# Gate stores on ScalarE's queue, respaced key and value products, state rows at another place, and one bias product for four heads

## The chip, the cores and the metric

The kernel runs on one core of a Trainium2 chip. The core has TensorE (PE, with PEld for its weight loads), VectorE (DVE), ScalarE (ACT), GpSimd (POOL) and SyncE (SP), and 16 DMA engines that move data between DRAM and on-chip memory. DMAs are issued here from SP's queue, from POOL's and, in places, from ACT's. The metric is the device time of one execution in microseconds. The kernel before took 2555.72 us in the median of three runs (2555.23 to 2556.82).

## The reference

The kernel computes one layer of a hybrid mixer for a prompt of 2048 rows and for 64 sample rows (8 sequences of 8 new rows each, with cached keys and values). The parts that the change touches are these:

```python
z = einsum('btd,de->bte', rms_norm(x, g_norm), w_in)          # one wide product, cut into
xa, ga, q, k, v, gb, gm = split(z, [o1, o2, o3, o4, o5, o6])  # recurrence, attention, gates
xa, new_conv = causal_conv(xa, conv_buf, conv_w, conv_b)      # new_conv is an output
hs, h_last = rg_lru(xa, h0, ...)                              # h_last is an output
for g in range(3):                    # windows 128, 512, 2048; dilations 1, 4, 16; 4 heads each
    bias = rel_bias[t5_bucket(arange(129) * DILATIONS[g]), g * 4:(g + 1) * 4]
    # prompt: 128 queries against 256 keys in the band, score * scale + bias[distance]
    # sample: 64 queries, each against 129 keys of its cache, then P @ cached values
    o, lse, nb = dilated_group(q[g], k[g], v[g], cache[g], bias, DILATIONS[g])
alpha = softmax(stack(lses), axis=0)                          # merges the three groups
yb = einsum((sum(alpha * outs) * silu(gb)), w_attn_proj)
gates = sigmoid(gm + b_merge)                                 # 2 x 1024 columns
merged = gates[..., :1024] * ya + gates[..., 1024:] * yb
y = x + einsum(merged, w_out)
```

## The kernel before, in words

Everything is written out by hand: each engine executes its list in the order in which the program emits it, and an instruction that waits holds all that stand behind it on its engine. The same holds for each engine's list of DMA issues. The hardware DMAs, from SP and from ACT alike, use eight semaphores in turn, so a DMA also waits until the one that last used its semaphore has landed.

A product of full precision is three matmul passes: the 24 matmuls of `zT` (line 757 on) take eight slices of the depth and, for each, the high weight part with the high input part, the low part with the high one, and the high one with the low input part (RH, RL).

*The attention stage* (64 to 1134 us of the trace) goes through 12 heads (groups 2, 1, 0), each in 17 units `ph`, one per 128 rows. In the unit loop the weights of the next head `nh` are loaded and converted, and its bias is made: `bias_0` (ph 7) loads the one-hot table of the group and lets POOL broadcast one column of `reln` to 128 columns, `bias_a` (ph 9) multiplies the two on PE to 128 equal rows of 383 values, copies them on ACT and stores them in the DRAM table `Dsc`, and `bias_b` (ph 12) loads two skewed views of it as the tile T. The first head's come at unit 0.

*The recurrence stage* (1134 to 1659 us) makes the recurrent branch. Its last block is finished inside the next stage.

*The gate stage* (1659 to 2078 us) goes over 16 blocks `f` of 128 gate columns (`gm_block`, line 991 on). A block is five chunks of 512, 512, 384, 384 and 320 rows. In each chunk PE makes the product z, hooks run, ACT makes the gate tile `gt` (sigmoid; two buffers in the blocks from 1 on), the tile is stored to DRAM (`Gsc`), and one piece of the cache is copied (`copy`). z takes turns in a few PSUM tiles, so PE waits when ACT has not emptied an old one. The weights of block f+1 are split into a high and a low part on ACT and DVE in chunk 0 of block f (`nextw`), and the raw weights of f+2 are loaded (`nextr`, line 680) into a single buffer, which that split has just read.

From block 1 on, each chunk then also does a step t of `plan` (line 1268 on), a table of lists of functions: the attention of the sample rows. Step t stands in chunk 6 + t, counted from the stage's start. In it are:
- the key products: `G.kq.go`, two products of 128 x 128 on DVE for each call; `kts` lists the steps of the calls (four a step from step 2, three from 20 to 23), and `kl` is the step behind the last;
- the multiplications of cached values: `v2_load` (SP, line 1152), `v2_mul` (ACT, four per tile, line 1156), `v2_acc` (DVE), and the like for group 1, spread over steps 6 to 66; a load goes out some four tiles ahead into six buffers;
- the products of the remaining values, `v_conv(i)` (ACT and POOL split a tile) and one step later `v_mm(i)` (PE, tile OT, line 1221), at the steps `mmt`, every second from `kl + 7`;
- the small tables `SA` (scores, lines 1062 and 1065), the queries `qs`, softmax and merge steps.

The state rows of the recurrence (`states`) are made by a hook in the last chunk of block 0: PE transposes the columns `par`, the last of which POOL writes (lines 927 and 928), DVE copies them, and SP stores four outputs. The tile `hs` lies where block 0's pools end.

*The output stage* (2078 us to the end) projects the attention, merges and multiplies by the last weights.

The functions that the diff touches, and what calls them:

Of the kernel before, what the change touches and what calls it, by code (L numbers as in the profile page):

```python
# [11 lines left out]
F32 = mybir.dt.float32  # L12
# [30 lines left out]
def program(tc, I, O, C, upto=99, debug=False):  # L43
# [13 lines left out]
    else:  # L57
        sd = lambda n, s, dt=F32: dram.tile(s, dt, name=n)
    Dsc = sd("Dsc", [12, 128, NBX])
    Osc = sd("Osc", [3, SEQ, 4, 130])  # L60
    QS = sd("QS", [3, NS, 512])
    SK = sd("SK", [3, NS, 2, 4, HD])
# [212 lines left out]
    heads = [(g, h) for g in (2, 1, 0) for h in range(4)]  # L275
    Wt, Wr, Tt = {}, {}, {}

    def bias_0(g, h):
        hd = g * 4 + h
        oh = ap_.tile([128, NBX], F32, name="oh", tag="wraw", bufs=4)  # L280
        dma(oh[0:33, :], C["onehot"][:, g, :])
        lb = ap_.tile([128, HD], F32, name="lb", tag="kqs", bufs=1)
        POOL.tensor_copy(lb[0:33, :], reln[:, hd:hd + 1].to_broadcast([33, 128]))
        G.ohlb = oh, lb

    def bias_a(g, h):
        hd = g * 4 + h
        oh, lb = G.ohlb
        eb = ps.tile([128, NBX], F32, name="eb", tag="op")
        PE.matmul(eb, lb[0:33, :], oh[0:33, :], start=True, stop=True)  # L290
        es_ = ap_.tile([128, NBX], F32, name="es_", tag="wraw", bufs=4)
        ACT.copy(es_, eb)
        dma(Dsc[hd], es_)

    def bias_b(g, h):
        hd = g * 4 + h
# [202 lines left out]
    x_mul(1, D // 2, D)  # L499
    POOL.tensor_scalar(gq, gq, -SCALE, 0.0, ALU.mult, ALU.add)  # L500
    POOL.tensor_scalar(reln[0:32, :], reln[0:32, :], -1.0, 0.0, ALU.mult, ALU.add)
    bias_0(*heads[0])
    w_conv(heads[0], 6, DVE)
    w_conv(heads[0], 7, DVE)
    N = len(units)
# [30 lines left out]
    for i in range(N + 3):  # L536
# [82 lines left out]
        if u:  # L619
            if i < 15:  # L620
                x_mul(i + 2, 0, D // 2)
            if i > 50 and i // 17 in (3, 7) and ph < 16:
                x_mul(ph, 0, D // 2)
            if i == 0:
                bias_a(*heads[0])
                bias_b(*heads[0])
        if nh:
            if ph == 7:
                bias_0(*nh)
            if ph == 9:  # L630
                bias_a(*nh)
            if ph == 12:
                bias_b(*nh)
            if ph == 11:
                for k in range(4):
                    w_load(nh, k)
            if ph == 13:
                w_conv(nh, 0, POOL)
                w_conv(nh, 1, DVE)
                w_load(nh, 4)  # L640
                w_load(nh, 5)
# [257 lines left out]
    def tail_2(b):  # L899
        for c0, n in CH:  # L900
            s = slice(c0, c0 + n)
            ACT.activation(rr[:, s], rr[:, s], AF.Exp, scale=c8[:, b:b + 1])
            a2 = lp.tile([128, 512], F32, name="a2", tag="ii", bufs=2)
            POOL.tensor_mul(a2[:, 0:n], rr[:, s], rr[:, s])
            DVE.scalar_tensor_tensor(tt[:, s], a2[:, 0:n], 1.0, tt[:, s], ALU.add, ALU.mult)

    def tail_r(b):
        for c0, n in CH:
            ACT.activation(tt[:, c0:c0 + n], tt[:, c0:c0 + n], AF.Sqrt)

    def tail_3(b, i0=0, i1=5):
        for c0, n in CH[i0:i1]:
            s = slice(c0, c0 + n)
            DVE.tensor_mul(xc[:, s], xc[:, s], tt[:, s])
            if c0 + n == NT:
                a0 = rr[:, SEQ:NT:8]
                hh = lp.tile([128, 8], F32, name="hh", tag="hh")
                DVE.tensor_mul(hh, a0, par[:, b, 34:42])
                DVE.tensor_add(xc[:, SEQ:NT:8], xc[:, SEQ:NT:8], hh)
                DVE.memset(a0, 0.0)  # L920
            init = 0.0 if c0 == 0 else tt[:, c0 - 1:c0]
            DVE.tensor_tensor_scan(tt[:, s], rr[:, s], xc[:, s], init, ALU.mult, ALU.add)
            POOL.tensor_mul(sgl[:, s], sgl[:, s], tt[:, s])
            dma(Y1[b][:, s], sgl[:, s])
        if i1 < 5:
            return
        POOL.tensor_copy(par[:, b, 4:5], tt[:, SEQ - 1:SEQ])
        POOL.tensor_copy(par[:, b, 34:42], tt[:, SEQ + 7:NT:8])
# [46 lines left out]
        POOL.tensor_copy(par[:, b, 0:3], xpad[:, SEQ:SEQ + 3])  # L975
        POOL.tensor_copy(par[:, b, 10:34].rearrange("p (s j) -> p s j", j=3), xsp[:, :, 8:11])

    def states():
        hs = lp.tile([42, 1024], F32, name="hs", tag="xh")
        for i in range(2):  # L980
            hp = ps.tile([42, 512], F32, name="hp", tag="tr")
            for k in range(4):
                PE.transpose(hp[:, k * 128:(k + 1) * 128], par[:, i * 4 + k, :], ident)
            DVE.tensor_copy(hs[:, i * 512:(i + 1) * 512], hp)
        for a, b, d in ((0, 3, O["conv_p"][0, 0]), (4, 5, O["h_p"][0]), (10, 34, O["conv_s"][0].rearrange("b j d -> (b j) d")), (34, 42, O["h_s"][0])):
            dma(d, hs[a:b, :])


    mg = ExitStack()
    tasks = []  # L990
# [1 line left out]
    def gm_block(f, w, hooks, gtile):  # L992
        for ci, (c0, n) in enumerate(CH):
            z = ztile("z", "S")
            zT(z, w, c0, n)
            for h in hooks.get(ci, ()):
                h()
            gt = gtile()
            ACT.activation(gt[:, 0:n], z[:, 0:n], AF.Sigmoid, bias=par[:, f % 8, 8 + f // 8:9 + f // 8])  # L999
            dma(Gsc[f][:, c0:c0 + n], gt[:, 0:n])  # L1000
            copy()
            if plan and f:
                for fn in plan.pop(0):
                    fn()
# [4 lines left out]
    def nextw(f):  # L1009
        if f + 1 < 16:  # L1010
            wm[f + 1] = w_split(G.wr, DVE)

    def nextr(f):
        if f + 2 < 16:
            G.wr = w_raw(wcols(C_GM + (f + 2) * 128))

    G.wr = wgr
    gm_block(0, wm[0], {0: (lambda: nextw(0), lambda: nextr(0), lambda: tail_2(7)), 1: (lambda: tail_r(7), lambda: tail_3(7, 0, 2)), 2: (lambda: tail_3(7, 2, 5),), 4: (states,)},
             lambda: lp.tile([128, 512], F32, name="gt0", tag="ii", bufs=2))
    lr.close()  # L1020
    gts = ExitStack()
# [34 lines left out]
    def sload(g):  # L1056
        SA = SAs[g] = mp.tile([NS, 4, 192], F32, name="SA", tag="SA", bufs=2)
        br = SA[:, :, 0:128]
        o = g * 4 * 128 * NBX + 127
        if g == 0:  # L1060
            for h in range(4):
                dma(br[:, h], raw(Dsc, o + h * 128 * NBX, [[0, 8], [NBX - 1, 8], [1, 128]]))
        else:
            dma(br, raw(Dsc, o, [[0, NS], [128 * NBX, 4], [1, 128]]))
        dma(SA[:, :, 128:192], SN[g * 4:g * 4 + 4].rearrange("h p k -> p h k"))
# [185 lines left out]
    def s_out2():  # L1251
# [7 lines left out]
        for a in range(2):  # L1259
            nc.gpsimd.dma_start(Y2v[:, a * 4:a * 4 + 4, SEQ:NT], yt[:, a])  # L1260

    sload(2)
    sload_k(2)
    prep()
# [8 lines left out]
    P = lambda f, *a: lambda: f(*a)  # L1273
    kts = []
    while len(kts) < G.kq.left:
        t = kts[-1] if kts else 2
        kts.append(t + (kts.count(t) == (3 if 20 <= t < 24 else 4)))
    kl = kts[-1] + 1
    mmt = [kl + 7 + 2 * i for i in range(NI_)]
    for i, (g, b, r) in enumerate(items):  # L1280
        if b is None and i:
            at_(mmt[i] - 1, P(s_evac, items[i - 1][0]), P(soft_b, g))
# [2 lines left out]
    for i in range(NI_):  # L1285
        at_(mmt[i] - 1, P(v_conv, i))
    T = mmt[-1]
    at_(1, G.kq.init, G.kq.queries)
    at_(2, P(scores, 2), P(news, 2, range(4)), P(sload, 1), P(sload_k, 1))
    at_(3, P(soft_a, 2))  # L1290
    at_(4, v2_p)
# [301 lines left out]
```

## Time and profile before

| | |
|---|---|
| median of three runs | 2555.72 us (2555.23 to 2556.82) |
| profiled execution | 2556.18 us |
| its span in the trace | 2554.4 us |
| PE busy | 2493.1 us (98%) |
| DVE busy | 1546.4 us (61%) |
| ACT busy | 1081.5 us (42%) |
| POOL busy | 557.9 us (22%) |
| DMA, mean | 147 GB/s |
| chain that ended last, share of PE | 83% |

The trace is of the profiled execution. Its times are microseconds from the start of the span; the span begins and ends a little inside the execution, which here adds 1.8 us. Busy time of an engine is the time in which it executes; idle time is followed by the name of what released it ("<-"). The granted clock is that of PE: 1.00 is 2.4 GHz and 0.50 is 1.2 GHz. A line number is that of the kernel's file; L93 and L94 are the two steps of a split into high and low parts, made by a helper for many tiles.

### The profile page before, as it was taken

The numbers are of one execution on the slowest core, as the hardware profiler recorded it, in microseconds if no ns is written. First come the engines' busy times: TensorE is split into PE (matmuls) and PEld (weight loads), VectorE is DVE, ScalarE is ACT, GpSimd is POOL, SyncE is SP. The second block draws the span as 40 slices with busy tenths as digits, with TensorE's granted clock in tenths as the row PEclk, the third lists the DMA queues.
The fourth block names the chain that finished last, engine by engine and source line by source line (L and its number), as shares of the span: only waits on it lengthen the run. The fifth ranks groups of instructions, "written<-read, shape, count | busy, mean of one in ns | idle before, by whom it ended". The sixth has DMA issues, their size and how long they took to land.

```text
span 2554.4 us, 44714 instructions
## 1 busy us (share of the span) xinstructions
PE 2493.1 (98%) x15196; PEld 2340.1 (92%) x15196; DVE 1546.4 (61%) x4805; ACT 1081.5 (42%) x3327; POOL 557.9 (22%) x897
## 2 busy tenths in 40 slices
PE   8999999999999999999999999999889999999999
PEld 7999999999999999999999999988778899988988
DVE  6744686777786776647676677638755723433322
ACT  5534454443454443444455655536466511211110
POOL 3423322222221221213233334320000012200000
PEclk9999999999999999999999999999999999999999
DMA  5443564554553433327644434355555479633332
GB/s 145 117 130 97 139 193 135 164 163 136 162 153 110 120 117 99 107 73 233 208 143 140 129 118 133 125 173 177 177 166 186 146 223 337 192 112 123 111 122 66
DMA packets 311288, 376.73 MB, mean 147 GB/s; under 512 B 54914, under 2 KB 254926, under 8 KB 308220
## 3 DMA queue, kind: packets, MB, share of 16 engines
q1 hardware_dynamic: 297028, 356.31, 45.7%
q0 software_dynamic: 14032, 17.57, 2.5%
q8 instruction: 120, 1.97, 0.3%
q14 instruction: 108, 0.88, 0.1%
HBM read 293.55 MB, written 168.31 MB: 181 GB/s over the span
## 4 chain that ended last, share of the span: by engine, by line
PE 83%; DMA 6%; DVE 5%; ACT 3%; issue 1%; SPq 1%; POOL 1%; DVEq 0%; ACTq 0%; POOLq 0%
PE z L336 28%; PE zt L760 22%; PE zt L1471 7%; PE zt L1503 7%; PE zt L534 3%; PE zt L1415 3%; PE zga L888 2%; DMA v<-in_cache_kv_w 2%; PE trx L247 1%; PE op L428 1%; PE S L406 1%; DVE kjk L178 1%; PE tre L416 1%; DMA xt<-in_x_prompt 1%; PE trc L376 1%
## 5 line engine op out<-in xcount | busy, mean ns | idle before, releaser
L336 PE MATMUL z<-w,RH 128*128 128x384 f32 (+1 forms) x3088 | 889.1, 349 | 6.1 <-POOL w L317 2.3
L760 PE MATMUL zt<-RH,wz 128*128 128x384 f32 (+2 forms) x2560 | 700.1, 356 | 12.9 <-ACT gt L999 12.0
L336 PEld LDWEIGHTS z<-w,RH 128*128 128x128 f32 (+1 forms) x3088 | 553.3, 188 | 16.1 <-POOL w L317 6.2
L336 PE MATMUL z<-w,RL 128*128 128x384 f32 x1544 | 520.5, 337 | 0.0
L760 PEld LDWEIGHTS zt<-RH,wz 128*128 128x128 f32 x2560 | 465.6, 190 | 58.8 <-ACT gt L999 14.2
L760 PE MATMUL zt<-RL,wz 128*128 128x384 f32 (+2 forms) x1280 | 454.1, 355 | 0.0
L336 PEld LDWEIGHTS z<-w,RL 128*128 128x128 f32 x1544 | 291.5, 189 | 0.7 <-DVE RL L94 0.4
L178 DVE CUSTOM_DVE_ANT_0 kjk<-kt,qs 128x128 bf16<-128x128 f32 x768 | 227.6, 296 | 63.1 <-DMA qs<-QS 27.7
L760 PEld LDWEIGHTS zt<-RL,wz 128*128 128x128 f32 x1280 | 242.4, 189 | 22.5
L408 ACT ACTIVATE P<-P,o 128x128 f32<-128x128 f32 (+1 forms) x192 | 88.9, 463 | 309.1 <-DVE o L407 309.1
L345 ACT ACTIVATE jk<-z 128x128 bf16<-128x128 f32 (+1 forms) x408 | 113.0, 277 | 236.5 <-PE trc L376 173.5
L94 DVE TENSOR_TENSOR KQ<-trc,KQ 128x256 fp32r<-128x256 f32 x192 | 81.4, 424 | 209.0 <-ACT KQ L93 209.0
L347 POOL TENSOR_SCALAR ss<-ss 128x2 f32<-128x2 f32 (+1 forms) x204 | 43.8, 215 | 714.5 <-ACT jk L345 671.2
L1471 PEld LDWEIGHTS zt<-y1t,w_wlo 128*128 128x128 f32 x1536 | 190.3, 191 | 0.6
L1471 PE MATMUL zt<-y1t,w_wlo 128*128 128x256 f32 (+1 forms) x1536 | 190.6, 286 | 0.0
L1503 PE MATMUL zt<-w_wo,mt 128*128 128x512 f32 x672 | 162.0, 395 | 0.0
L1503 PEld LDWEIGHTS zt<-w_wo,mt 128*128 128x128 f32 x672 | 126.1, 188 | 30.6
L348 POOL TENSOR_TENSOR rs<-ss,neghalf 128x2 f32<-128x2 f32 (+1 forms) x204 | 142.7, 699 | 17.0
L1156 ACT ACTIVATE v<-v,P 128x128 f32<-128x128 f32 x256 | 81.2, 391 | 77.7 <-DMA v<-in_cache_kv_w 68.9
L434 DVE TENSOR_REDUCE o<-op 128x128 f32<-128x256 f32 x192 | 80.6, 420 | 44.2 <-PE op L429 44.0
L1505 DVE TENSOR_TENSOR xr<-zt,xr 128x512 f32<-128x512 f32 (+1 forms) x34 | 23.5, 692 | 137.3 <-PE zt L1503 132.6
L93 ACT CAST mt<-g 128x256 fp32r<-128x256 f32 x72 | 27.2, 388 | 187.2 <-DVE g L1474 172.1
(292 smaller groups left out, 4259.3 us busy)
## 6 DMA issues: line engine op xcount, KB each, us to landing
out_kv_s<-in_cache_kv_w SPq DMA_DIRECT2D x176, 480.0 KB
xt<-in_x_prompt SPq DMA_DIRECT2D x48, 512.0 KB
wr<-in_w_in SPq DMA_DIRECT2D x96, 192.0 KB
kt<-in_cache_kv_w SPq DMA_DIRECT2D x128, 128.0 KB
wzr<-in_w_in SPq DMA_DIRECT2D x32, 512.0 KB
v<-in_cache_kv_w SPq DMA_DIRECT2D x128, 128.0 KB
Osc<-o SPq DMA_DIRECT2D x192, 65.0 KB
ot<-Osc SPq DMA_DIRECT2D x32, 390.0 KB
```

Source lines behind the costliest of these rows:

```text
L94: eng.tensor_sub(l, src, h.bitcast(F32))
L178: DVE.tensor_tensor_reduce(jk, kts[q.tile][:, c], qts[t][:, c], 1.0, 0.0, ALU.mult, ALU.add, q.SC[:, o:o + 1])
L336: PE.matmul(u.z[0:m, :], (RH, RL, RH)[p][:, k, u.cols], Wt[(u.g, u.h), k][:, (0, 0, 1)[p], :], start=(i == 0), stop=(i == 23))
L345: ACT.activation(jk[0:m, :], z[0:m, i * 128:(i + 1) * 128], AF.Square, accum_out=u.ss[0:m, i:i + 1])
L348: POOL.tensor_tensor(u.rs[0:m, :], u.ss[0:m, :], neghalf[0:m, :], ALU.pow)
L408: ACT.activation(u.P[:, 0:n], u.P[:, 0:n], AF.Exp, bias=u.o[:, 128:129], scale=-1.0, accum_out=u.o[:, 129:130])
L434: DVE.tensor_reduce(u.o[:, 0:128], u.op.rearrange("p a b -> p b a"), AX.X, ALU.add)
L534: PE.matmul(z[0:m, 0:256], (RH, RH, RL)[p][:, k, j * 128:j * 128 + m], wb[c * 8 + k][:, (0, 1, 0)[p], :], start=(i == 0), stop=(i == 23))
L760: PE.matmul(z[:, 0:n], w[:, (0, 1, 0)[p], k, :], (RH, RH, RL)[p][:, k, c0:c0 + n], start=(i == 0), stop=(i == 23))
L1156: ACT.activation(v2s[n][:, h], v2s[n][:, h], AF.Copy, scale=P2[:, h, n:n + 1])
L1471: PE.matmul(z[:, 0:n], wl[k][:, (0, 1, 0)[p], f, :], y1s[c * 8 + k][:, (0, 0, 1)[p], 0:n], start=(i == 0), stop=(i == 23))
L1503: PE.matmul(z[0:m, :], ms_[k][:, (0, 0, 384)[p] + o:(0, 0, 384)[p] + o + m], wo[k][:, (0, 1, 0)[p], e * 4:(e + 1) * 4, :].rearrange("p k c ...
```

## The change

There are four edits.

The first is the bias. `bias_0(g)` and `bias_a(g)` run once for each group, ahead of its first head: one product of the four columns of `reln` (no broadcast) with the one-hot table gives four rows, which ACT copies and SP stores in a new DRAM table `Esc`. `bias_c(g, h)`, for every head at ph 10 (and for the first head at unit 0), is a DMA from DRAM to DRAM that writes 128 copies of a row of `Esc` into `Dsc`. `bias_b` is as before.

The second is `states`: no hook of block 0 any more, but steps 1 and 2 of `plan` (block 1's second and third chunk), half in each, with a tile of the sample's pool and its four stores issued by POOL.

The third is the store of a gate tile: `ACT.dma_start` in place of SP's `dma`.

The fourth is the table of steps: key products three a step from step 3 (3 to 45, `kl` 46, before 2 to 34 and 35), and value products at 53, 55, 56 to 63 and 65 instead of every second step from 42 to 62.

```diff
--- before.py
+++ after.py
@@ -57,6 +57,7 @@
     else:
         sd = lambda n, s, dt=F32: dram.tile(s, dt, name=n)
     Dsc = sd("Dsc", [12, 128, NBX])
+    Esc = sd("Esc", [12, NBX])
     Osc = sd("Osc", [3, SEQ, 4, 130])
     QS = sd("QS", [3, NS, 512])
     SK = sd("SK", [3, NS, 2, 4, HD])
@@ -275,22 +276,21 @@
     heads = [(g, h) for g in (2, 1, 0) for h in range(4)]
     Wt, Wr, Tt = {}, {}, {}
 
-    def bias_0(g, h):
+    def bias_0(g):
+        G.oh = ap_.tile([128, NBX], F32, name="oh", tag="wraw", bufs=4)
+        dma(G.oh[0:33, :], C["onehot"][:, g, :])
+
+    def bias_a(g):
+
+        eb = ps.tile([4, NBX], F32, name="eb", tag="op")
+        PE.matmul(eb, reln[:, g * 4:g * 4 + 4], G.oh[0:33, :], start=True, stop=True)
+        es_ = ap_.tile([128, NBX], F32, name="es_", tag="wraw", bufs=4)
+        ACT.copy(es_[0:4, :], eb)
+        dma(Esc[g * 4:g * 4 + 4], es_[0:4])
+
+    def bias_c(g, h):
         hd = g * 4 + h
-        oh = ap_.tile([128, NBX], F32, name="oh", tag="wraw", bufs=4)
-        dma(oh[0:33, :], C["onehot"][:, g, :])
-        lb = ap_.tile([128, HD], F32, name="lb", tag="kqs", bufs=1)
-        POOL.tensor_copy(lb[0:33, :], reln[:, hd:hd + 1].to_broadcast([33, 128]))
-        G.ohlb = oh, lb
-
-    def bias_a(g, h):
-        hd = g * 4 + h
-        oh, lb = G.ohlb
-        eb = ps.tile([128, NBX], F32, name="eb", tag="op")
-        PE.matmul(eb, lb[0:33, :], oh[0:33, :], start=True, stop=True)
-        es_ = ap_.tile([128, NBX], F32, name="es_", tag="wraw", bufs=4)
-        ACT.copy(es_, eb)
-        dma(Dsc[hd], es_)
+        dma(Dsc[hd], raw(Esc, hd * NBX, [[0, 128], [1, NBX]]))
 
     def bias_b(g, h):
         hd = g * 4 + h
@@ -499,7 +499,7 @@
     x_mul(1, D // 2, D)
     POOL.tensor_scalar(gq, gq, -SCALE, 0.0, ALU.mult, ALU.add)
     POOL.tensor_scalar(reln[0:32, :], reln[0:32, :], -1.0, 0.0, ALU.mult, ALU.add)
-    bias_0(*heads[0])
+    bias_0(heads[0][0])
     w_conv(heads[0], 6, DVE)
     w_conv(heads[0], 7, DVE)
     N = len(units)
@@ -622,13 +622,16 @@
             if i > 50 and i // 17 in (3, 7) and ph < 16:
                 x_mul(ph, 0, D // 2)
             if i == 0:
-                bias_a(*heads[0])
+                bias_a(heads[0][0])
+                bias_c(*heads[0])
                 bias_b(*heads[0])
         if nh:
-            if ph == 7:
-                bias_0(*nh)
-            if ph == 9:
-                bias_a(*nh)
+            if ph == 7 and nh[1] == 0:
+                bias_0(nh[0])
+            if ph == 9 and nh[1] == 0:
+                bias_a(nh[0])
+            if ph == 10:
+                bias_c(*nh)
             if ph == 12:
                 bias_b(*nh)
             if ph == 11:
@@ -975,16 +978,6 @@
         POOL.tensor_copy(par[:, b, 0:3], xpad[:, SEQ:SEQ + 3])
         POOL.tensor_copy(par[:, b, 10:34].rearrange("p (s j) -> p s j", j=3), xsp[:, :, 8:11])
 
-    def states():
-        hs = lp.tile([42, 1024], F32, name="hs", tag="xh")
-        for i in range(2):
-            hp = ps.tile([42, 512], F32, name="hp", tag="tr")
-            for k in range(4):
-                PE.transpose(hp[:, k * 128:(k + 1) * 128], par[:, i * 4 + k, :], ident)
-            DVE.tensor_copy(hs[:, i * 512:(i + 1) * 512], hp)
-        for a, b, d in ((0, 3, O["conv_p"][0, 0]), (4, 5, O["h_p"][0]), (10, 34, O["conv_s"][0].rearrange("b j d -> (b j) d")), (34, 42, O["h_s"][0])):
-            dma(d, hs[a:b, :])
-
 
     mg = ExitStack()
     tasks = []
@@ -997,7 +990,7 @@
                 h()
             gt = gtile()
             ACT.activation(gt[:, 0:n], z[:, 0:n], AF.Sigmoid, bias=par[:, f % 8, 8 + f // 8:9 + f // 8])
-            dma(Gsc[f][:, c0:c0 + n], gt[:, 0:n])
+            ACT.dma_start(Gsc[f][:, c0:c0 + n], gt[:, 0:n])
             copy()
             if plan and f:
                 for fn in plan.pop(0):
@@ -1015,7 +1008,7 @@
             G.wr = w_raw(wcols(C_GM + (f + 2) * 128))
 
     G.wr = wgr
-    gm_block(0, wm[0], {0: (lambda: nextw(0), lambda: nextr(0), lambda: tail_2(7)), 1: (lambda: tail_r(7), lambda: tail_3(7, 0, 2)), 2: (lambda: tail_3(7, 2, 5),), 4: (states,)},
+    gm_block(0, wm[0], {0: (lambda: nextw(0), lambda: nextr(0), lambda: tail_2(7)), 1: (lambda: tail_r(7), lambda: tail_3(7, 0, 2)), 2: (lambda: tail_3(7, 2, 5),)},
              lambda: lp.tile([128, 512], F32, name="gt0", tag="ii", bufs=2))
     lr.close()
     gts = ExitStack()
@@ -1259,6 +1252,17 @@
         for a in range(2):
             nc.gpsimd.dma_start(Y2v[:, a * 4:a * 4 + 4, SEQ:NT], yt[:, a])
 
+    def states(i):
+        if i == 0:
+            G.hs = mp.tile([128, 1024], F32, name="hs", tag="vt2", bufs=VB[1])
+        hp = ps.tile([42, 512], F32, name="hp", tag="tr")
+        for k in range(4):
+            PE.transpose(hp[:, k * 128:(k + 1) * 128], par[:, i * 4 + k, :], ident)
+        DVE.tensor_copy(G.hs[0:42, i * 512:(i + 1) * 512], hp)
+        if i:
+            for a, b, d in ((0, 3, O["conv_p"][0, 0]), (4, 5, O["h_p"][0]), (10, 34, O["conv_s"][0].rearrange("b j d -> (b j) d")), (34, 42, O["h_s"][0])):
+                POOL.dma_start(d, G.hs[a:b, :])
+
     sload(2)
     sload_k(2)
     prep()
@@ -1273,10 +1277,12 @@
     P = lambda f, *a: lambda: f(*a)
     kts = []
     while len(kts) < G.kq.left:
-        t = kts[-1] if kts else 2
-        kts.append(t + (kts.count(t) == (3 if 20 <= t < 24 else 4)))
+        t = kts[-1] if kts else 3
+        kts.append(t + (kts.count(t) == 3))
     kl = kts[-1] + 1
-    mmt = [kl + 7 + 2 * i for i in range(NI_)]
+    mmt = [kl + 7]
+    for g, b, r in items[1:]:
+        mmt.append(mmt[-1] + (2 if b is None else 1))
     for i, (g, b, r) in enumerate(items):
         if b is None and i:
             at_(mmt[i] - 1, P(s_evac, items[i - 1][0]), P(soft_b, g))
@@ -1285,7 +1291,10 @@
     for i in range(NI_):
         at_(mmt[i] - 1, P(v_conv, i))
     T = mmt[-1]
+    assert T + 1 < 68
     at_(1, G.kq.init, G.kq.queries)
+    for i in range(2):
+        at_(1 + i, P(states, i))
     at_(2, P(scores, 2), P(news, 2, range(4)), P(sload, 1), P(sload_k, 1))
     at_(3, P(soft_a, 2))
     at_(4, v2_p)
```

The order of PE's list at the bias of the second head, in the attention stage (z is the head's product, eb the bias, trc and tre transposes). Before:

```order
L336 MATMUL z<-w,RL 128x384
L336 MATMUL z<-w,RH 128x384 x2
L336 MATMUL z<-w,RL 128x384
L336 MATMUL z<-w,RH 128x384
L290 MATMUL eb<-oh,lb 128x383
L376 MATMUL trc<-ident,kvo 128x128
L377 MATMUL trc<-ident,qn 128x128
L416 MATMUL tre<-ident,P 128x128
```

and after the change, at the same place:

```order
L336 MATMUL z<-w,RH 128x384
L336 MATMUL z<-w,RL 128x384
L336 MATMUL z<-w,RH 128x384 x2
L336 MATMUL z<-w,RL 128x384
L336 MATMUL z<-w,RH 128x384
L376 MATMUL trc<-ident,kvo 128x128
L377 MATMUL trc<-ident,qn 128x128
```

The bias product of that head is gone and nothing stands in its place; the rest is as it was.

SP's list of issues in the gate stage, up to the scores' tables of group 0 in step 16 (Gsc is a gate store, v a tile of cached values, kt of keys, qs of queries, SA a table of scores; the numbers behind v are those of its tiles in the program). Before:

```order
L1000 DMA Gsc<-gt 128x512
L1152 DMA v_22033<-in_cache_kv_w 64x1x512 x2
L1152 DMA v_22036<-in_cache_kv_w 64x1x512 x2
L155 DMA kt<-in_cache_kv_w 128x1x512
L145 DMA qs<-QS 128x1x512 x2
L1062 DMA SA<-Dsc 64x1x128 x4
L1065 DMA SA<-SN 64x4x64
L1000 DMA Gsc<-gt 128x384
L1152 DMA v_22092<-in_cache_kv_w 64x1x512 x2
```

and after:

```order
L1145 DMA v_21874<-in_cache_kv_w 64x1x512 x2
L1145 DMA v_21921<-in_cache_kv_w 64x1x512 x2
L1145 DMA v_21924<-in_cache_kv_w 64x1x512 x2
L156 DMA kt<-in_cache_kv_w 128x1x512
L1055 DMA SA<-Dsc 64x1x128 x4
L1058 DMA SA<-SN 64x4x64
L1145 DMA v_21974<-in_cache_kv_w 64x1x512 x2
L1145 DMA v_22021<-in_cache_kv_w 64x1x512 x2
```

The gate stores are out of SP's list, and the other issues stand in their order; the queries come at another step.

ACT's list at about the same steps of the gate stage (gt is a gate tile, v a multiplication of four heads' values). Before:

```order
L1156 ACTIVATE v_21933<-v_21933,P_21164 128x128 x4
L999 ACTIVATE gt<-zt,par 128x384
L1156 ACTIVATE v_21984<-v_21984,P_21164 128x128 x4
L1156 ACTIVATE v_22033<-v_22033,P_21164 128x128 x4
L999 ACTIVATE gt<-zt,par 128x384
L1156 ACTIVATE v_22036<-v_22036,P_21164 128x128 x4
```

and after:

```order
L993 DMA Gsc<-gt 128x512
L1149 ACTIVATE v_21825<-v_21825,P_21073 128x128 x4
L992 ACTIVATE gt<-zt,par 128x384
L993 DMA Gsc<-gt 128x384
L1149 ACTIVATE v_21874<-v_21874,P_21073 128x128 x4
L1149 ACTIVATE v_21921<-v_21921,P_21073 128x128 x4
L992 ACTIVATE gt<-zt,par 128x384
```

Each gate tile is now followed by the issue of its store, ahead of the multiplications of its step; their number in a step is as before.

## Rows read from the trace of the kernel before

**Rows 1.** Windows by stage: stretch, length, busy us of each engine (instructions), clock, DMA share, GB/s.

```profile
64.00:1134.00 1070.00, 1060.22 (x6696) 1026.67 (x6695) 730.34 (x2840) 470.62 (x1944) 264.56 (x543) 1.00 0.46 131
...
1659.18:2077.81 418.63, 387.22 (x1998) 347.38 (x1997) 251.72 (x901) 214.34 (x550) 31.62 (x48) 0.96 0.53 168
```

**Rows 2.** Waits of PE, gate stage: engine, line, releaser, total us, times, longest.

```profile
PE OT L1221 <- DVE vt L94: 12.2, 1, 12.2
PE zt L760 <- ACT gt L999: 12.0, 5, 5.4
PE hp L983 <- POOL par L928: 5.3, 1, 5.3
```

**Rows 3.** Timeline of PE, gate stage: start, us, instruction, [idle before, releaser].

```profile
1731.11 0.62 PE L760 MATMUL zt<-RH,wz 128*128 128x384 f32 x2 [1.59 <-ACT gt L999]
...
1807.01 1.01 PE L760 MATMUL zt<-RH,wz 128*128 128x384 f32 x2 [5.36 <-ACT gt L999]
...
1810.70 0.52 PE L760 MATMUL zt<-RL,wz 128*128 128x384 f32 x1
1811.02 0.84 PE L760 MATMUL zt<-RH,wz 128*128 128x384 f32 x2
...
1811.88 0.51 PE L760 MATMUL zt<-RH,wz 128*128 128x384 f32 x2
```

**Rows 4.** Groups of ACT, gate stage: line, shapes, count, busy, mean ns, idle before.

```profile
L1156 ACT ACTIVATE v<-v,P 128x128 f32<-128x128 f32 x256 | 81.2, 391 | 77.7 <-DMA v<-in_cache_kv_w 68.9 <-DVE SCk L178 6.9 <-DVE V L1162 1.5
...
L999 ACT ACTIVATE gt<-zt,par 128x384 f32<-128x384 f32 x32 | 18.2, 570 | 42.1 <-DMA Gsc<-gt 27.8 <-PE zt L760 9.6 <-issue 4.7
L93 ACT CAST wz<-wzr 128x1024 fp32r<-128x1024 f32 x15 | 15.5, 1034 | 0.0
```

**Rows 5.** Waits of ACT, gate stage.

```profile
ACT gt L999 <- DMA Gsc<-gt: 37.0, 9, 14.1
```

**Rows 6.** Waits of SP's queue, gate stage.

```profile
SPq L1000 <- ACT gt L999: 100.8, 37, 8.1
SPq L680 <- DVE wz L94: 50.1, 10, 16.2
```

**Rows 7.** Timeline of PE around a bias product, attention stage.

```profile
166.81 0.91 PE L290 MATMUL eb<-oh,lb 33*128 33x383 f32 x2
167.64 0.33 PE L376 MATMUL trc<-ident,kvo 128*128 128x128 f32 x1
```

**Rows 8.** Timeline of SP's queue and DVE, the first head's bias.

```profile
21.86 0.33 SPq L293 DMA_DIRECT2D Dsc<-es__238  x1
24.21 0.32 SPq L298 DMA_DIRECT2D T<-Dsc  x1
24.58 0.42 SPq L299 DMA_DIRECT2D T<-Dsc  x1
...
29.29 0.28 DVE L401 TENSOR_TENSOR P<-S,T 128x128 f32<-128x128 f32 x1
```

**Rows 9.** Timeline of POOL: a column of par, a split of values.

```profile
1688.05 0.19 POOL L928 COPY par<-tt 128x8 f32<-128x8 f32 x1
...
1949.86 1.47 POOL L94 TENSOR_TENSOR vt<-vr,vt 128x512 fp32r<-128x512 f32 x1 [17.22 <-ACT vt L93]
```

**Rows 10.** Timeline of ACT, gate stage.

```profile
1684.67 0.58 ACT L999 ACTIVATE gt<-zt,par 128x384 f32<-128x384 f32 x1 [5.16 <-DMA Gsc<-gt]
...
1805.27 1.28 ACT L1156 ACTIVATE v<-v,P 128x128 f32<-128x128 f32 x4 [7.98 <-DMA v<-in_cache_kv_w]
...
1901.70 1.28 ACT L1156 ACTIVATE v<-v,P 128x128 f32<-128x128 f32 x4 [5.94 <-DMA v<-in_cache_kv_w]
```

**Rows 11.** Timeline of SP's queue, gate stage.

```profile
1682.16 0.39 SPq L1000 DMA_DIRECT2D Gsc<-gt  x1
...
1890.29 4.87 SPq L1054 DMA_DIRECT2D SCt<-SCs  x8
```

**Rows 12.** Groups of DVE, gate stage.

```profile
L178 DVE CUSTOM_DVE_ANT_0 kjk<-kt,qs 128x128 bf16<-128x128 f32 x256 | 74.5, 291 | 42.4 <-DMA qs<-QS 27.4 <-DMA kt<-in_cache_kv_w 7.3
```

## Prediction

> **What bounds the kernel now.** I read the busy time by stage first. In the attention stage TensorE (PE) is busy 1060.22 of 1070.00 us [rows 1], so the time there is the length of PE's own list, and only work taken off PE shortens it. In the gate stage, from the first gate product to the first product of the attention projection, PE is busy 387.22 of 418.63 us: 31.4 us stand idle, and the granted clock averages 0.96 there, against 1.00 in the attention stage [rows 1]. So this stage has two kinds of loss, and the list of PE's waits says where the idle part is [rows 2]: 12.2 us once, before the first sample product OT, which waits for its converted values; 12.0 us in five waits for a gate tile, that is for ScalarE (ACT) to empty a product; 5.3 us once for the state columns, which POOL writes last; the rest is small.
>
> The clock part is read from single products [rows 3]. After 5.36 us of idling two 384-wide products and the one after them take 0.84 and 0.52 us, and from 1811.88 on two take 0.51 us: the lower level (1.2 GHz for 2.4) from 1807.01 to about 1811.7, half of which is lost, 2.3 us. A wait of 1.59 us, before 1731.11, is not followed by it. The five waits of line 760 are 1.6, 1.5, 5.4, 2.5 and 1.0 us in order of time (their sum is the row's 12.0 [rows 2]). I count 2 us of clock behind each wait of 2.5 us or more, of which there are four: 8 us, an estimate from the one stretch shown. Idle and clock together: 39.4 us, the most that this stage can give.
>
> Then why ACT is late. Its groups show 77.7 us of idling before the multiplications of the cached values v, 68.9 of them for the loads, and its waits 37.0 us, in nine times, for the landing of a gate store [rows 4, 5]. The sync engine (SP) issues both in one list: it stood 100.8 us at line 1000 for ACT to finish a gate tile and 50.1 us at the weight load for VectorE (DVE) [rows 6]; while it stands, the v loads behind stand too.
>
> **The bias, four heads in one product.** The product and the next instruction start 0.83 us apart (166.81 to 167.64) [rows 7]. Nine of twelve go: 9 x 0.83 = 7.5 us, all of it on PE, which has no slack there to lose it in. The four-row product still streams 383 columns, so the remaining three are taken at the same price. Nine ACT copies and POOL copies go with them, off the path. The broadcasts of the later heads have two units between issue and use, some 11 us if the stage's 1070 us are shared by its 200 units or so [rows 1]; that hides them. Only the first head pays: its bias now makes one more trip through memory. A store issued at 21.86 let the dependent load go at 24.21, 2.35 us [rows 8]. The load's second half was issued 24.58 and used at 29.29; with the same 2.35 us for landing that left 2.4 us, and the new trip takes about all of it. Next late would be the input tile queued behind it. Bounds 0 and 2.35 us; I take 0.5, near the lower end, since the slack is as long as the trip.
>
> **The state rows moved.** They stood on PE behind the last recurrence and cost 5.35 us and 2.0 us of clock. In their new place, after the second product of the next block, POOL's last column (written at 1688.05 [rows 9]) is done before PE arrives, two products of 512 columns after the old place. The transposes and copies themselves move unchanged; their four stores go from SP to POOL's queue, idle then. ACT no longer waits for them to land before its first gate tile of the new block. Gain 7.4 us; if the copies fell behind other DVE work nobody on PE waits for them.
>
> **Gate stores on ACT's queue.** Eighty issues leave SP, and with them its 100.8 us of waiting for ACT. What is late next: a store now takes its turn in ACT's list. A store issued 1682.16 let the waiting gate tile start 1684.67, so issue and landing are about 2.5 us [rows 10, 11]; a tile is used again two chunks later, 9 us, so the landing is hidden and the 37.0 us of gate waits go. ACT's need per chunk: gate tile 0.57, v in 96 steps of four over 60 chunks 1.6 x 1.28 (four in a row overlap, as the row at 1805.27 shows) = 2.05, weight cast 1.03/5 = 0.21: 2.8 us [rows 4, 10]. A chunk takes PE (418.6 - 31.4 - 8)/80 = 4.74 us. 1.9 us are spare. No row of before shows an issue on ACT: bounds 0 and, by the dearest issue on SP, 4.87/8 = 0.61 us; I take the 0.39 of a gate store there [rows 11], inside the spare. But a DMA also waits for the one that last used its semaphore, which now couples ACT's stores to SP's loads: a store can hold ACT until a v load two places ahead has landed, which it would have waited for one multiplication later anyway. And early, SP's small tables now wait for gate stores of the block's first four chunks, some 6 us later than before, an estimate from PE's 4.74 us a chunk; DVE's list no longer has key products ahead of the first softmax of the sample, which is worth more than that: four pairs waited there for the query tiles.
>
> Here the Trainium skill speaks against the change: "DMA: Bandwidth & Descriptors", section "Issuing engines are not separate DMA queues", says that issuing from several engines saves only the sequencer's issue time. By it the edit saves 80 x 0.39 = 31 us of SP and nothing on PE. The trace agrees that the loads, more than the stores, hold ACT (68.9 against 37.0 us), but not that issue time is all that one list costs, as its 100.8 us at line 1000 show.
>
> **Products respaced.** Key products go from four to three a chunk: a step is two products of 291 ns [rows 12], so DVE's share falls from 2.3 to 1.7 us of a 4.74 us chunk, and the weight split behind it, on which SP's next loads wait, comes sooner. The stage's later sample steps move eleven chunks back, and eight OT products follow each other at every chunk instead of every second. Between two, ACT's gate tile 0.57, store 0.39, a cast of about the same width as a gate tile 0.6, POOL's split 1.47 [rows 9] and its two small copies, under 0.6, take 3.6 us; PE takes 4.74, less at a narrow chunk. Hidden while ACT is not late; if it is, each waits. Bounds 0 and 8 x 1 us; I take 0 and keep the other end for the range.
>
> **The sum of the stage's waits.** Of 39.4 us the states took 7.4; 32.0 are left. I keep the two small waits before 1731 and 1774 (3.1 us), since the burst of small loads at the stage's start is unchanged; 1 us of those between 1800 and 1850 (8.7 us and 4 of clock), since both followed long v waits of ACT (7.98 us before 1805.27) behind SP's list; and of the 15.7 us around the first OT, where ACT had lost 5.94 us to v behind eight table loads (4.87 us of SP) [rows 10, 11], 5.9. Left: 10.0, gone: 22.0.
>
> Sum: 7.5 - 0.5 + 7.4 + 22.0 = 36.4 us. The profiled execution took 2556.18 us, 1.8 outside its span; 2556.2 - 36.4 = 2519.8, and the median is 0.5 lower: 2519. I say 2520, and by the spread of each term 2512 to 2531.
>
> **Rivals.**
> 1. The loads stay late. The v loads wait for DVE's sums and land when they land; the stores never set ACT's pace. Then only the bias and the states gain: 2556.2 - 7.0 - 7.4 = 2541.8, say 2541. For it: 68.9 us of load waits; against it: each long one follows a stretch in which SP stood at a gate store or a weight load. The page's rule above would end here too.
> 2. Nothing is left idle: 2556.2 - 7.0 - 39.4 = 2509.8, less 0.5: 2509. For it: 1.9 us spare a chunk; against it: the first OT is behind ACT's list with no tile of slack.
> 3. Slower: the store holds ACT for its landing, because its semaphore's last DMA is always still under way. Place: ACT's list, chunks 6 to 66; price: 2.5 us and 0.39 of issue, 2.9 - 1.9 spare = 1.0 us x 60 = 60 us, against 46.4 to gain: 2556 - 46 + 60 = 2570. It decides from a hold of 1.9 + 46/60 = 2.7 us per store. Against it: eight semaphores in turn, on which SP's eight table loads of before were issued in 4.87 us [rows 11].
> 4. The bias edit does not do what it says, because its slot on PE was filled with other idling anyway: 7.5 us less gain, 2527, inside the likeliest range. Against it: PE's 1060 of 1070 us.
>
> **Chances.** Forecast with rival 4: 0.60. Rival 1: 0.20. Rival 2: 0.13. Rival 3: 0.05; a gain eaten to nothing by several: 0.02. The range goes from 2508, below the floor of rival 2, to 2543, just past rival 1; outside lie rival 3 and a tail. 0.2% (5 us) is about what a measurement of this kernel tells from no change. Faster by more: 0.60 + 0.20 + 0.13 = 0.93; within: 0.03; slower: 0.04.
>
> **What would show it.** Right: no wait for the state columns; ACT's gate tiles wait for no store; SP's wait for ACT's gate tiles is gone; 24 eb products become 6; PE idle in the gate stage under 15 us, clock above 0.98. Wrong: ACT's waits for v stay near 69 us (rival 1), rows of ACT's queue held at the stores beyond 1.9 us each (rival 3), or waits before several OT products in a row, which would say that the closer spacing is not covered.

## The result, and the profile after

The changed kernel took 2538.77 us in the median of four runs (2537.17 to 2542.17), the kernel before 2556.27 beside it: a ratio of 0.9934, 95% interval 0.9916 to 0.9951. That is 17.5 us less. The forecast was 2520, 36.4 us less; the time lies inside the stated range of 2508 to 2543, near its upper end. The profiled execution took 2537.17 us, its span 2535.4; the stages below are of that one, which is 19.0 us shorter than the profiled execution before.

By stages, in the columns of [rows 1] (the gate stage now runs from 1651.87 to 2061.30):

```profile
64.00:1127.00 1063.00, 1052.85 (x6696) 1026.79 (x6695) 731.96 (x2845) 469.00 (x1944) 263.85 (x536) 1.00 0.47 132
...
1651.87:2061.30 409.43, 386.88 (x1998) 348.00 (x1997) 247.85 (x901) 218.36 (x550) 33.58 (x52) 0.97 0.55 176
```

The gate stage begins 7.3 us earlier (1659.18 to 1651.87): the bias. It is 9.2 us shorter (418.63 to 409.43), where the forecast had 7.4 for the states and 22.0 for the waits. The other 2.5 us came behind it (476.59 to 474.10), where the first product no longer waits 2 us for its input tile. PE still idles 22.6 us in the gate stage, before 31.4, and the granted clock is 0.97, before 0.96; the forecast had asked for under 15 us and over 0.98. PE's waits there, against [rows 2]:

```profile
PE zt L763 <- ACT gt L992: 8.6, 4, 3.6
PE OT L1214 <- DVE vt L95: 6.8, 1, 6.8
PE zt L763 <- DVE wz L95: 5.6, 1, 5.6
PE OT L1214 <- POOL Z L1204: 1.6, 1, 1.6
```

The wait for the state columns is gone, the gate tiles' and the first sample product's are smaller, and the 5.6 us for a block's converted weights were 0.8. What ACT waits for (line 1149 is v, 992 the gate tile), against [rows 4, 5], and what SP's queue waits for, against [rows 6]:

```profile
ACT v L1149 <- DMA v<-in_cache_kv_w: 52.4, 20, 13.5
...
ACT gt L992 <- DMA Gsc<-gt: 2.6, 5, 1.1
```

```profile
SPq L683 <- DVE wz L95: 29.5, 9, 4.8
SPq L683 <- DMA Gsc<-gt: 24.3, 2, 23.9
...
SPq L110 <- DMA Gsc<-gt: 9.3, 3, 5.6
SPq L1145 <- DMA Gsc<-gt: 8.7, 6, 1.9
...
SPq L146 <- DMA Gsc<-gt: 6.3, 2, 5.1
...
SPq L1047 <- DMA Gsc<-gt: 6.1, 3, 2.4
```

ACT's 37.0 us for the landing of stores are all but gone, as forecast, and so are SP's 100.8 us for gate tiles. But SP now waits for the *landing* of gate stores, at weight loads (683), copies (110), v loads (1145), query loads (146) and score tables (1047), none of which reads a gate store: with seven smaller rows 72.6 us. Line 1363 among them (6.1 us) does read one, and about 16 of the longest wait stand as a wait for DVE in a run below; some 50 us are new. So one wait took the place of another. The trace names the semaphore of each DMA: SP's and ACT's issues carry the same eight numbers (100 to 102, 104 to 108), POOL's eight others (111 to 118). A load of SP that waits for a gate store waits for the number that this store carries.

The coupling works in the other direction too. Five gate stores could not go out at once, because the last DMA of SP on their number was still under way, and ACT stood with them, 5.3 us together. The longest, in ACT's timeline:

```profile
1896.26 0.56 ACT L992 ACTIVATE gt<-zt,par 128x384 f32<-128x384 f32 x1
1899.20 0.33 ACTq L993 DMA_DIRECT2D Gsc<-gt  x1
1899.65 1.28 ACT L1149 ACTIVATE v<-v,P 128x128 f32<-128x128 f32 x4 [2.83 <-DMA kt<-in_cache_kv_w]
```

The store goes out 2.4 us after its tile is done, and what ends the wait is the load of a key tile, which ACT does not read.

### The profile page after: what moved, and what is told of

The parts are those of the page before. It is cut to its first block, busy times and chain, and to the rows that moved or that the text cites. A ratio compares the mean times of both kernels' runs of the same rounds, so it can differ in the third digit from the quotient of the medians.

```text
span 2535.4 us, 44585 instructions
## 1 busy us (share of the span) xinstructions
PE 2482.5 (98%) x15178; PEld 2337.5 (92%) x15178; DVE 1543.3 (61%) x4805; ACT 1081.6 (43%) x3318; POOL 557.1 (22%) x889
## 5 line engine op out<-in xcount | busy, mean ns | idle before, releaser
L1149 ACT ACTIVATE v<-v,P 128x128 f32<-128x128 f32 x256 | 80.7, 390 | 78.7 <-DMA v<-in_cache_kv_w 52.4
```

The lines of the kernel that those rows point to most:

```text
L1149: ACT.activation(v2s[n][:, h], v2s[n][:, h], AF.Copy, scale=P2[:, h, n:n + 1])
```

## Experiments

Each run was compared with the kernel before on its own chip (medians 2555.8 to 2556.8). I held three theories for the missing gain: L, the loads are late by themselves (the forecast's first rival); S, ACT's stores take turns on the semaphores of SP's loads; I, the stores' issue costs ACT time.

**One edit at a time on the kernel before.** The bias (the first edit of the diff, whole):

> The kernel before with one edit: the bias of four heads in one product. The forecast's step: 7.5 - 0.5 us, 2549 to 2550, all of it ahead of the gate stage. If the slot on PE was filled anyway: 2555 to 2557.

2546.02 us, ratio 0.9952 (0.9937 to 0.9968): 10.8 us less, 3 us beyond the range of the step. Its gate stage begins at 1650.32, 8.9 us earlier. The second case falls; the step is right in kind, and if anything small.

The states (the second edit, whole):

> The kernel before with one edit: the state rows made in steps 1 and 2 of the plan. The forecast's step: 5.35 us of waiting and 2 of clock, 2548 to 2550. If ACT's wait for the gate store or the sums behind it end last anyway: 2553 to 2557.

2554.22 us, ratio 0.9993 (0.9982 to 1.0004): 2.6 us, possibly nothing, as the second case had it. PE and ACT in its timeline, and SP's queue:

```profile
1715.56 0.79 PE L760 MATMUL zt<-RH,wz 128*128 128x512 f32 x1 [4.00 <-ACT gt L988]
```

```profile
1714.93 0.58 ACT L988 ACTIVATE gt<-zt,par 128x384 f32<-128x384 f32 x1 [20.87 <-DMA Gsc<-gt]
```

```profile
1698.86 8.13 SPq L1141 DMA_DIRECT2D v<-in_cache_kv_w  x12
1707.10 0.40 SPq L680 DMA_DIRECT2D wzr<-in_w_in  x1
1707.60 0.76 SPq L989 DMA_DIRECT2D Gsc<-gt  x1
```

The 5.35 us before the states are gone, and PE stands 4.00 us at the next late thing: ACT waits 20.9 us for a gate store that stands in SP's list behind tables and twelve v loads. That wait was there before; PE's wait for the states had covered it.

The stores alone (the third edit, whole):

> The kernel before with one edit: the gate stores issued by ACT. The forecast's own theory (the stores free SP's list): some 20 us less, 2536. Theory L (the loads of cached values are late whatever queue the stores take): no change, 2553 to 2558. Theory S (ACT's stores take turns on the eight semaphores of SP's loads, so that SP's waits for gate tiles turn into waits for stores to land): a small gain or loss, 2548 to 2558, and SP shows tens of us of waits for the landing of gate stores, which theory L doesn't ask for.

2566.26 us, ratio 1.0040 (1.0025 to 1.0055): 10 us *slower*, outside all three ranges. ACT's stores and SP's loads of constants at the start of the stage:

```profile
1695.00 0.33 ACTq L1000 DMA_DIRECT2D Gsc<-gt  x1
...
1700.31 0.33 ACTq L1000 DMA_DIRECT2D Gsc<-gt  x1
...
1704.36 0.33 ACTq L1000 DMA_DIRECT2D Gsc<-gt  x1
...
1708.52 0.33 ACTq L1000 DMA_DIRECT2D Gsc<-gt  x1
```

```profile
1697.72 0.47 SPq L1036 DMA_DIRECT2D relb<-in_rel_bias  x1
1702.34 0.47 SPq L1037 DMA_DIRECT2D NI<-c_ni  x1
1706.23 0.47 SPq L1038 DMA_DIRECT2D MK<-c_mk  x1
1710.38 0.37 SPq L1039 DMA_DIRECT2D SEL<-c_sel  x1
```

Four loads that depend on nothing go out 1.9 to 2.7 us behind four stores, one per chunk, and each carries and waits for the semaphore number of the store ahead of it (108, 100, 101, 102): SP runs at ACT's pace. In the run with the states alone, where SP issues the stores, the first and last of the four stand at 1695.63 and 1698.16. Behind them the queries come late, DVE stands for them, the key products stand ahead of the first softmax (sm) on DVE, and ACT waits 25.5 us for it:

```profile
1732.20 0.29 DVE L178 CUSTOM_DVE_ANT_0 kjk<-kt,qs 128x128 bf16<-128x128 f32 x1 [22.15 <-DMA qs<-QS]
```

```profile
1735.73 0.46 ACT L1088 ACTIVATE SA<-SA,sm 64x192 f32<-64x192 f32 x1 [25.50 <-DVE sm L1086]
```

All gate stores of this run go out as soon as their tiles are done; what holds is SP's list, not ACT's.

The table of steps (the fourth edit, whole), alone and with the stores:

> The kernel before with one edit: the new table of steps for key and value products. The forecast's theory: nothing by itself, 2553 to 2558, since SP's list is held by gate stores as before. Theory L: the key products leave DVE sooner to the sums, so buffers come free sooner: up to 5 us less, 2551 to 2556. A loss of over 3 us (2559 or more) would say that the closer value products are not covered.

2551.65 us, ratio 0.9981 (0.9972 to 0.9991): 5.0 us, in theory L's range, where the forecast had none.

> The kernel before with two edits: gate stores issued by ACT, and the new table of steps. If the two add up: 2566.3 - 5.0 = 2561. Theory K (ACT's stores alone lost time because SP's tables and queries came late while the key products stood ahead of the first softmax, which held ACT 25.5 us and PE 9.8; the new table takes them out of its way): that wait goes, with its clock, 2546 to 2554.

2552.86 us, ratio 0.9988 (0.9978 to 0.9998). The two don't add up: ACT's wait at the softmax is down from 25.5 us to 0.9, and the stores' loss from 10 us to 1.2, which is inside the intervals.

```profile
1710.75 0.46 ACT L1088 ACTIVATE SA<-SA,sm 64x192 f32<-64x192 f32 x1 [0.94 <-DVE sm L1086]
```

PE's 9.8 us there are gone, though it stands 4.2 us at a block's weights and 3.2 at a gate tile soon after. Theory K holds: the new table makes the stores' move bearable.

**The changed kernel with the stores on another queue.** By SP, and by POOL:

```diff
-            ACT.dma_start(Gsc[f][:, c0:c0 + n], gt[:, 0:n])
+            POOL.dma_start(Gsc[f][:, c0:c0 + n], gt[:, 0:n])
```

> The changed kernel, but the gate stores are issued by SP again. The forecast's theory: the gain of the stores is lost, 2555 to 2562. Theory L: no change, 2535 to 2542. Theory S: SP waits for the gate tiles in place of the landings, within 5 us of the changed kernel either way, 2534 to 2544.

2542.13 us, ratio 0.9943 (0.9928 to 0.9958). So in the changed kernel the stores on ACT are worth 3.4 us against SP, inside the noise of the two; 22 had been forecast. (SP's waits for gate tiles are back, 96.0 us.)

> The changed kernel, but the gate stores are issued by POOL, whose DMAs have semaphores of their own. Theory S: SP's waits for the landing of gate stores (some 70 us in the gate stage of the changed kernel) go, and PE's waits of 22.6 us there fall to about 10: 2525 to 2530. Theory L: loads as late as before, 2535 to 2542.

2520.59 us, ratio 0.9860 (0.9843 to 0.9876): 18.2 us less than the changed kernel, more than theory S had expected. Theory L falls as the account of the missing gain, though ACT still waits 43.6 us for v. Its gate stage, PE's waits in it and two of ACT's:

```profile
1652.57:2044.80 392.23, 382.85 (x1999) 345.64 (x1998) 249.10 (x901) 213.96 (x550) 75.15 (x131) 0.98 0.56 184
```

```profile
PE zt L763 <- ACT gt L992: 6.1, 2, 5.0
PE OT L1214 <- DVE vt L95: 3.3, 1, 3.3
```

```profile
ACT v L1149 <- DMA v<-in_cache_kv_w: 43.6, 13, 8.7
...
ACT gt L992 <- DMA Gsc<-gt: 26.7, 13, 8.1
```

In SP's list no load waits for a gate store any more but line 1363, which reads one (5.6 us); the weight load's longest wait is 16.1 us, for DVE. PE idles 9.4 us against 22.6. ACT's waits for the landing of a gate store are back (26.7 us, 2.6 in the changed kernel), and the run is the faster one all the same: those waits were not what the time hung on. But POOL's queue also takes the issue off ACT, so theory I is still in it. Two runs part them. A copy on ACT of about the issue's time:

```diff
+            ACT.activation(gt[:, 0:256], gt[:, 0:256], AF.Copy, scale=1.0)
             POOL.dma_start(Gsc[f][:, c0:c0 + n], gt[:, 0:n])
```

> The run with gate stores issued by POOL, and one more ACT operation behind each gate tile (256 of its columns copied onto themselves), some 0.45 us, the time that a store's issue took in ACT's list. Theory I (what the stores cost on ACT is their issue time, 80 x 0.45 = 36 us of ACT): as slow as the changed kernel, 2535 to 2542. Theory S (it is the semaphores shared with SP's loads): 2519 to 2526.

2528.85 us, ratio 0.9886 (0.9871 to 0.9900): 8.3 us, between the two ranges. The two intervals touch, but the executions of the two runs lie apart (2525.0 to 2530.3 against 2519.3 to 2522.5). The copies take ACT 418 ns each; with one, the next operation starts some 0.45 us later than without, against some 0.56 us with a store's issue (below), so the copy is a little too short a stand-in:

```profile
L993 ACT ACTIVATE gt<-gt 128x256 f32<-128x256 f32 x79 | 33.0, 418 | 2.5
```

And a small DMA in the store's turn, without the copy:

```diff
+            ACT.dma_start(Jsc[f * 5 + ci], ident[0:1, 0:64])
             POOL.dma_start(Gsc[f][:, c0:c0 + n], gt[:, 0:n])
```

> The run with gate stores issued by POOL, and a DMA of 256 bytes issued by ACT behind each gate tile, into a table that nobody reads. Theory S: the small DMA takes a semaphore in its turn just as the store did, so SP's loads wait for ACT's list again: 2532 to 2542, with SP waiting tens of us for its landing. A theory by which the volume or the landing time of the store matters: 2519 to 2526. Theory I: 2532 to 2542 as well, but then the run with the copy on ACT is as slow.

2531.61 us, ratio 0.9902 (0.9887 to 0.9916): 11.0 us, at the lower edge of theory S's range. SP's waits (684 is the weight load, 928 a store of the branch, 111 a copy; with five smaller rows 46.1 us, of which some 16 of the longest stand as a wait for DVE where ACT issues nothing):

```profile
SPq L684 <- DMA Jsc<-ident: 20.5, 1, 20.5
...
SPq L928 <- DMA Jsc<-ident: 12.6, 3, 5.1
...
SPq L111 <- DMA Jsc<-ident: 3.8, 1, 3.8
```

256 bytes that nobody reads hold SP's loads just as a gate store does, so it is the turn on the semaphore, not the volume. Where the small DMA waits for nothing, its issue takes no time of ACT: it goes out while four multiplications run on without a gap.

```profile
1745.46 0.41 ACT L1151 ACTIVATE v<-v,P 128x128 f32<-128x128 f32 x1 [0.69 <-DMA v<-in_cache_kv_w]
1745.68 0.20 ACTq L994 DMA_DIRECT2D Jsc<-ident  x1
1745.77 0.98 ACT L1151 ACTIVATE v<-v,P 128x128 f32<-128x128 f32 x3
```

But in eight places it waits for a load of SP that carries its semaphore number, and ACT stands with it, 13.6 us together. Here 3.5 us, for a key tile that ACT does not read:

```profile
1870.53 0.56 ACT L993 ACTIVATE gt<-zt,par 128x384 f32<-128x384 f32 x1
1874.61 0.20 ACTq L994 DMA_DIRECT2D Jsc<-ident  x1
1874.93 2.46 ACT L1151 ACTIVATE v<-v,P 128x128 f32<-128x128 f32 x8 [3.84 <-DMA kt<-in_cache_kv_w]
```

So the 11.0 us are the price of the shared turn in both directions, SP held by ACT and ACT held by SP; no run parts the two.

With both additions:

> The run with gate stores by POOL, with both additions at once: the copy on ACT and the small DMA issued by ACT. If ACT's time (8.3 us alone) and the shared semaphores (11.0 alone) are two costs that add up, and together all that ACT's stores cost: 2520.6 + 19.3 = 2540, as the changed kernel, 2536 to 2543. If they are two views of one delay: 2529 to 2534, and some 7 us of the changed kernel's loss have a third cause.

2538.94 us, ratio 0.9936 (0.9916 to 0.9956): the two costs add up (2520.6 + 8.3 + 11.0 = 2539.9), and together they are the changed kernel's 2538.8. No third cause is needed, within the 5 us or so that the intervals leave open.

**What the other edits are worth once SP is free.**

> The kernel before with one edit: gate stores issued by POOL. Theory S: the forecast's step was right for a queue of its own, and fails with ACT's: 22 us less, 2530 to 2540. If the stores free nothing without the other edits: 2550 to 2557.

2545.73 us, ratio 0.9959 (0.9943 to 0.9974): 10.1 us, between the two. With the old table the first softmax still holds ACT (13.2 us) and the first sample product PE (10.9 us).

> The run with the changed kernel's other edits and gate stores by POOL, with the old table of steps. If the new table is worth the same 5 us as in the kernel before: 2523 to 2528. If it gains only while SP's list is held: 2518 to 2522.

2532.92 us, ratio 0.9912 (0.9895 to 0.9930): the new table is worth 12.3 us here, more than both expected. The stores' queue and the table help each other. This run and the one before it differ by the bias and the states alone, 12.8 us; less the bias (7.3 to 10.8 us) that leaves 2 to 5.5 for the states once the stores are off SP's list.

The last two runs move one split:

```diff
-        at_(mmt[i] - 1, P(v_conv, i))
+        at_(mmt[i] - (1 if i else 2), P(v_conv, i))
```

> The run with gate stores by POOL, and the split of the first sample values one step earlier, so that ACT's delay has a chunk to be made up before PE's first sample product. If that product is where ACT's delay comes out: PE's 3.3 us there and 3 of clock go, 2512 to 2517. If the delay comes out at the next gate tile instead: 2518 to 2522.

2515.08 us, ratio 0.9838 (0.9817 to 0.9858), the fastest version tried. PE's waits:

```profile
PE zt L763 <- ACT gt L992: 4.5, 2, 3.0
PE OT L1214 <- DVE PN L95: 2.7, 1, 2.7
PE OT L1214 <- POOL Z L1204: 0.9, 2, 0.5
```

The first product no longer waits (the 2.7 us stand before the second), and the stage is 387.85 us long at a granted clock of 1.00. The intervals of this run and of the one without the early split overlap, so that the 5.5 us between them are likely, not shown.

> The changed kernel, with the split of the first sample values one step earlier. If the wait before the first sample product (6.8 us, and clock behind it) is ACT's delay coming out at one place, with ACT's stores too: 2529 to 2534. If ACT is late at the next gate tile as well: 2536 to 2541.

2535.99 us, ratio 0.9923 (0.9907 to 0.9939): 2.8 us less than the changed kernel, at the lower edge of the second range, with intervals that overlap. With ACT's stores PE waits at other products instead: 9.7 us for gate tiles, against 8.6, and 3.6 us at the second sample product.

## Why the prediction was wrong, step by step

**The bias: right.** 7.0 us forecast; the stage begins 7.3 us earlier in the changed kernel and 8.9 in the run with that edit alone, whose median is 10.8 us less. The four-row product costs as much as a broad one, as taken: 482 ns a record, six of them, against 534 for the 24 before. What the first head's longer trip costs, taken as 0.5 us, stays open: PE's waits in the first 64 us are 12.8 us in the changed kernel, before 10.8, which would be near the upper bound of 2.35, but 10.5 in the run with this edit alone (there at a granted clock of 0.95, against 1.00 in the other two).

**The states: wrong.** 7.4 us forecast, 2.6 with an interval that includes none. "Nobody on PE waits for them" held; what the step did not name is what is late next, ACT behind a store in SP's list. The wait [rows 5] was in the profile (14.1 us, the longest); I counted it among the gains of the stores and not as what comes late next here. That PE's wait for the states had covered it is read from the two traces, not tested by a run.

**Gate stores on ACT's queue: the step that failed.** It said that "the landing is hidden and the 37.0 us of gate waits go", which happened, and that with SP's waits for ACT gone 22.0 us of PE's waits go with them; the move gave 3.4. Two terms were mis-sized:
- The semaphores, 11.0 us. The step saw that the turn "couples ACT's stores to SP's loads", and priced both directions at nothing: a store held by a load would have waited "one multiplication later anyway", and loads held by stores it named only for the small tables at the stage's start. But eight DMAs behind each store a DMA of SP, all through the stage, waits until ACT, however late, has issued that store and it has landed. SP's 100.8 us of waiting for gate tiles in its own list became waits for the landings of the same tiles' stores, some 50 us of them new. Of ACT's own holds, five with 5.3 us, three were for v loads, as the step had it, one for a block's raw weights, and the longest for a key tile, which ACT would not have waited for.
- ACT's time, 8.3 us. I took 0.39 us a store "inside the spare" of 1.9 us a chunk. With the store's issue the next operation mostly starts about 0.46 us after the gate tile's end, and without it, in the run with POOL's stores, about 0.10 us before that end: some 0.56 us a store, still inside the spare. But the spare is a mean. ACT stands long at a few loads (13.5 us once in the changed kernel) and then has several chunks to make up; in those, as I read it, each store is on the path. The run with the copy shows the 8.3 us, not the chunks in which they are lost.

```profile
1750.49 0.68 ACT L992 ACTIVATE gt<-zt,par 128x512 f32<-128x512 f32 x1
1751.20 0.33 ACTq L993 DMA_DIRECT2D Gsc<-gt  x1
1751.65 0.70 ACT L1149 ACTIVATE v<-v,P 128x128 f32<-128x128 f32 x2 [0.48 <-DMA v<-in_cache_kv_w]
```

and in the run with POOL's stores:

```profile
1757.04 0.58 ACT L992 ACTIVATE gt<-zt,par 128x384 f32<-128x384 f32 x1
1757.51 2.44 ACT L1149 ACTIVATE v<-v,P 128x128 f32<-128x128 f32 x8
```

**The respacing: taken at nothing,** worth 5.0 us alone and 12.3 with SP free. I bounded its loss (8 us) and not its gain.

**The rivals.** The first one's time, 2541, came near, for another reason: most of the missing gain is not in loads that are late by themselves, as the POOL run shows; ACT's waits for v fell from 68.9 us to 52.4 in the changed kernel and 43.6 there, and what is left of them may be late by itself. The rule of the Trainium skill ("DMA: Bandwidth & Descriptors", section "Issuing engines are not separate DMA queues"), that another issuing engine saves only the sequencer's time, came near the size of this move (3.4 us), but the runs don't agree with its reason: POOL's queue was worth 18.2 us more, of which 11.0 are the price of the shared semaphores and no issue time. The third rival had the mechanism, a hold through the semaphores, but put all of it in ACT's list, where the changed kernel shows 5.3 us; in SP's it shows some 50. The run with the stores alone, 2566 us, came near its 2570 with no store held on ACT's queue, by SP's list alone. That the POOL run ends at the forecast's 2520 does not save the sum: in it the respacing gives 12.3 us that the sum had at none.

## What to carry to other kernels

A DMA list is not free of another engine because its instructions are elsewhere: if the queues share completion semaphores in turn, as SP's and ACT's do here, the slower engine sets the pace of both, so ask for each queue what waits behind the moved DMA in both directions. When one of two waits close together is removed, price the gain by the difference to the second. Spare time as a mean over a stage covers nothing in the chunks in which the engine is catching up.

## What the runs showed of the hardware

Behind a DMA that ACT issues right after the operation that makes its data, ACT's next operation started about 0.46 us after that operation's end (issue 0.33), where without the DMA it started about 0.10 us before it; an issue that waited for nothing took 0.20 us beside running multiplications, without a gap. POOL issued its stores in about 0.54 us each, on an engine that the stage uses little (75 of 392 us busy, stores included).
